# Probabilities times values of two attention heads by turns on the column halves of the TensorE array, 128 queries at a time

## The chip, the cores and the metric

The kernel runs on one core of one Trainium2 chip. The metric is the device time of one execution in microseconds (us). Less is better.

## The reference, cut to what matters

The program is two layers of a hybrid backbone over 256 latent tokens and 256 context tokens with 1024 features. Each layer feeds three token mixers from one projection: neighbourhood attention (8 heads of 64), a bidirectional recurrence, and windowed attention with a sink (8 query heads, 2 key heads). A mixture of 16 experts follows. The change touches the last two lines of the attentions, where probabilities meet values:

```python
p = jax.nn.softmax(jnp.concatenate([s_nb, s_ctx], axis=-1), axis=-1).astype(v.dtype)
o = (jnp.einsum('brjqam,brajmhd->brjqhd', p_nb, v_nb)      # neighbourhood keys
     + jnp.einsum('bhrjql,blhd->brjqhd', p[..., n_nb:], vc))  # context keys
...
o = (jnp.einsum('bnqkgd,bnmkd->bnqkgd', p[..., :nloc], vb)   # window, the same form
     + jnp.einsum('bkgnql,blkd->bnqkgd', p[..., nloc:nloc + L], vc))
```

In layer 0 the context tokens also attend among themselves; in layer 1 only the latents are needed.

## The kernel before, in words

Heads are taken in four pairs (`hp`) by `na_attend` (line 703) and `wa_attend` (line 772). For a pair, the queries and keys are transposed and split in two parts, and one PSUM bank `psd` (`po`, tag "d", one buffer) collects the pair's output: head 0 (`par` 0) on partitions 0 to 63, head 1 on 64 to 127. `attend` (line 627) does one head. For each of two tiles of 128 latent queries (`t`) it computes scores against 512 keys (line 625, in PSUM `psa`), the softmax on VectorE and ScalarE (`softmax_rows`, lines 586 to 592), four transposes of the probabilities `P` (line 639, in PSUM `pst`) and a ScalarE copy into half of `pT` (line 640). Then four products with the values follow (line 642): 64 columns of values are the stationary operand and 256 queries of `pT` move. In layer 0 the context queries come next, in two products of 256 queries (line 656). `split_out` reads the pair's bank. Both operands are plain float32, so a product is two matmul records in the profile, each with a weight load of its own.

```python
for c in range(4):
    PE.matmul(po[pp, 256:512], vfn(c), pT[:, c], start=c == 0, stop=c == 3, tile_position=(0, 64 * par))
```

`tile_position=(0, 64 * par)` puts the product on one half of the array's columns. The other half is unused meanwhile, since a head's products follow one another. Layer 1's experts use both halves by turns: at line 1459 the inner loop runs over the two halves `c`, with 64 stationary and 512 moving columns, and at line 356 the first modulation vectors use four quarters.

A scheduler orders each engine's instructions. It places parts of the big projections (lines 243 to 245, three passes for each product) between the steps of the attention, so that TensorE has work while a softmax is under way. TensorE takes its instructions in the written order. The neighbourhood bias of a pair is loaded by SP (line 721, eight transfers into four slices of `bm`) on the queue that also carries the weights (line 215), and GpSimd adds a mask (line 725).

Of the kernel before, what the change touches and what calls it, by code (L numbers as in the profile page):

```python
# [76 lines left out]
def kernel(es, tc, A, out, dbg=None):  # L77
# [19 lines left out]
    def banks(**n):  # L97
        """the eight banks of PSUM, shared out anew"""
        if "pool" in pb:
            pb["pool"].__exit__(None, None, None)  # L100
        pb["pool"] = tc.tile_pool(name="ps", bufs=1, space=PSUM)
        pb["tiles"] = pb["pool"].__enter__()
        pb["n"] = n
# [10 lines left out]
    def ps_a(shape=(128, 512)):  # L114
        return bank("a", shape)
# [16 lines left out]
    # products of zeros keep the tensor engine at its full clock where it has to wait  # L132
# [9 lines left out]
    # the table of exponentials, loaded while the transfers run  # L142
# [6 lines left out]
    # silu of the two conditioning vectors, padded to 32 columns  # L149
# [8 lines left out]
    # sums the four row groups of the first modulation vectors  # L158
# [3 lines left out]
    # lower bounds of the forget gates: columns (direction, depth, head)  # L162
# [22 lines left out]
    def slot_queue(*extra):  # L185
        """buffers for weights in the order of their use, the longest unused first"""
        wst.clear()
        wst.extend([(wp, "raw")] * RAW_BUFS + [(pool, tag) for pool, tag in extra for _ in range(nbuf[tag])])
# [10 lines left out]
    def later():  # L199
        """for transfers that shall not get ahead of the weights so far"""  # L200
        return tc.issue_after(loads[-1].ins)

    def spare(tag, shape, dt=F32):
        """a buffer for weights that holds something else from now on"""
# [47 lines left out]
    def ada_group(l, g):  # L252
        """2048 columns of both rows of silu(c) @ w_ada + b_ada, a step for each 128 rows of w_ada"""
# [39 lines left out]
    def rstd_of(dst, ssq, n):  # L293
        """dst = (ssq / n + eps) ** -0.5"""
# [5 lines left out]
    def norm_rows(pool, xt):  # L300
        """xt over its root mean square"""
# [8 lines left out]
    def start(hp, tp, consume):  # L310
        """the first layer's make_hT and its first product, one block of 128 features after the other, with the
        block's modulation"""
# [109 lines left out]
    def gemm_cols(l, hT, cols0, toks):  # L422
        """transposed outputs: one [128 columns, tokens] bank for each 128-column block"""
# [12 lines left out]
    # Blocks of h = 1, 2, 4, ... tokens are merged in pairs. K holds a key times the product of the forget  # L436
    # gates from the token to its block's edge, Q a query times the product from the block's other edge, so
    # that K . Q at level h is the decayed score across the pair's middle; no product ever exceeds one.
    def hgrn(l, hT, ybT, hg_, hg, vv, take_v):
        full = l == 0  # L440
        T0 = 0 if full else 256
        with hg_:
# [20 lines left out]
            # two heads by turns  # L463
# [5 lines left out]
    def hgrn_head(l, hT, ybT, hg, vv, gw, h, full, T0):  # L469
# [5 lines left out]
        # forward keys, then backward keys; backward queries, then forward ones; so that with two strides  # L475
        # left blocks' forward keys and right blocks' backward ones (and the opposite queries) are one operand
# [17 lines left out]
        # diagonal: q . (kf + kb)  # L494
# [7 lines left out]
        for lv in range(9):  # L502
# [27 lines left out]
            if True:  # L530
                n = 256 // hs
                m0 = T0 // (2 * hs)
                # left blocks take the factor of the right one and right blocks that of the left one
# [35 lines left out]
    def head_rstd(pool, src, nh, wide=True):  # L569
        """[128, nh] inverse root mean squares of the heads of one token tile"""  # L570
# [10 lines left out]
    def softmax_rows(s_in, bm, init, nsk, P):  # L581
        """P = exp(s + bm - max) / sum, rows on partitions; the sink's logit (nsk its negative) joins maximum and sum"""
        m = sm.tile([128, 4], F32, name="smx", bufs=6)
        flat = P if len(P.shape) == 2 else P.rearrange("p a k -> p (a k)")
        # P = -(s + bm), m[0] = -max
# [8 lines left out]
    # A head's 64 dimensions fill the 128 rows as high and low parts of the queries against the high (then the  # L594
    # low) parts of the keys twice: two float32r passes for all four products.
    def stack_q(pool, ps, T0):
        """ps [128, tokens] two heads' queries, transposed"""
# [9 lines left out]
    def stack_k(pool, k, c0):  # L607
        """two heads' keys from column c0 of k [128, token tile, columns]"""
# [18 lines left out]
    def attend(l, pool, qT, kT, par, bms, init, nsk, vfn, po):  # L627
        """one head; po [64, tokens] of the pair's bank"""
        full = l == 0
        pp = slice(64 * par, 64 * par + 64)  # L630
        pT = pool.tile([128, 4, 256], F32, name="pT", bufs=2)
        for t in range(2):
            ps = ps_a((128, 2, 256))
            score(ps.rearrange("p a k -> p (a k)"), qT, kT, 2 + t, 512)
            P = pool.tile([128, 2, 256], F32, name="P", bufs=3, tag="P")
            softmax_rows(ps, bms[t], init, nsk, P)
            pt = ps_t((128, 4, 128))
            for c in range(4):
                PE.transpose(pt[:, c], P[:, c // 2, 128 * (c % 2):128 * (c % 2) + 128], ident)
            S.copy(pT[:, :, 128 * t:128 * (t + 1)], pt)  # L640
        for c in range(4):
            PE.matmul(po[pp, 256:512], vfn(c), pT[:, c], start=c == 0, stop=c == 3, tile_position=(0, 64 * par))
        if full:
            ps = ps_a((128, 2, 256))
            P = pool.tile([128, 2, 256], F32, name="P", bufs=3, tag="P")
            for t in range(2):
                score(ps[:, t], qT, kT, t, 256)
                softmax_rows(ps[:, t], C[:, CZER:CZER + 256], init, nsk, P[:, t])
            pt = ps_t((128, 2, 2, 128))
            for c in range(2):  # L650
                for t in range(2):
                    PE.transpose(pt[:, c, t], P[:, t, 128 * c:128 * (c + 1)], ident)
            pT = pool.tile([128, 4, 256], F32, name="pT", bufs=2)
            S.copy(pT[:, 0:2], pt.rearrange("p c t q -> p c (t q)"))
            for c in range(2):
                PE.matmul(po[pp, 0:256], vfn(c), pT[:, c], start=c == 0, stop=c == 1, tile_position=(0, 64 * par))
# [37 lines left out]
    # 64 copies of a layer's bias table: a row of 3719 elements further on is one key column to the left  # L694
# [8 lines left out]
    def na_attend(l, pool, yT, q, k, v):  # L703
        full = l == 0
        T0 = 0 if full else 256
        bm = pool.tile([128, 5, 256], F32, name="bm")       # zeros for the context keys, then two heads' biases
        G.memset(bm[:, 0], 0.0)
        for hp in range(4):
# [6 lines left out]
            for par in range(2):  # L715
                h = 2 * hp + par
                b2 = []
                for t in range(2):
                    i = 1 + 2 * par + t
                    for r in range(2):  # L720
# [5 lines left out]
                    b2.append(mk(bm, 0, [[256 * i, 2], [1, 256]]))  # L726
                attend(l, pool, qT[par], kT[par], par, b2, 3e38, None,
                       lambda c, h=h: v[:, c, 64 * h:64 * h + 64], po)
            split_out(yT, hp, po[:, T0:])

    def wa_inputs(l, hT, pool):
# [25 lines left out]
        def take_q(t, ps):  # L757
            # heads h and h + 4, which read the two key heads, side by side
# [13 lines left out]
    def wa_attend(l, pool, yT, q, k, v):  # L772
# [7 lines left out]
        for hp in range(4):  # L780
# [5 lines left out]
            for par in range(2):  # L786
                h = hp + 4 * par
                attend(l, pool, qT[par], kT[par], par, bms, sk[:, h:h + 1], sk[:, h:h + 1],
# [906 lines left out]
```

## Time and profile before

| | us |
|---|---|
| median of three runs | 1803.81 (1800.16 to 1805.40) |
| profiled execution, span from the first to the last instruction | 1791.0 |
| median of the runs less that span (launch and end around it) | 12.8 |
| attention of layer 0 | 395 to 590 |
| attention of layer 1 | 1325 to 1475 |
| PE busy over the span | 1675.2 |
| DVE busy over the span | 1049.5 |

The profile gives no time of its own for what lies around the span of the profiled execution; the difference to the median of the runs stands for it. A busy row of PE counts a matmul until its last column has left the array, so neighbouring matmuls overlap in it. What a matmul holds up is read from the distance of starts.

### The profile page before, as it was taken

To read this page: it belongs to the slowest core of one execution; us is meant where nothing else is said; L and a number is where in the kernel's file an instruction comes from. 1 tells how busy PE (TensorE), PEld (TensorE's weight loads), DVE (VectorE), ACT (ScalarE), POOL (GpSimd) and SP (SyncE) were. 2 spreads that over 40 slices of the span, in tenths; PEclk is the share of its full clock that TensorE was granted. 3 is DMA by queue.
4 is the path that set the end of the run, shared out by engine and by line. 5 is a ranking of instruction groups with operands and counts; after the bars stand their busy time and mean duration, and the time that the engine had idled before them with its cause. 6 is when DMAs were issued, how large, how long until landed. Compare 5 with 4: busy or idle time off the path is not lost. (4 is left out here: it accounts for less than half of the span.)

```text
span 1791.0 us, 23658 instructions
## 1 busy us (share of the span) xinstructions
PE 1675.2 (94%) x8656; PEld 1218.1 (68%) x8657; DVE 1049.5 (59%) x1907; ACT 813.7 (45%) x1351; POOL 342.9 (19%) x343
## 2 busy tenths in 40 slices
PE   8999999999999999499999987999999999799997
PEld 4657677886676888477877765878877888433332
DVE  4328473447876345788888888588558766401101
ACT  3313332346676432377877874434456764201100
POOL 0003130322300134311321113133313202100000
PEclk8999999999999999699999997999999999899999
DMA  9795748432210455599999951432424348899996
GB/s 294 282 316 173 265 156 286 134 100 65 59 48 24 118 201 178 184 328 373 360 331 370 357 187 66 125 89 82 148 85 118 88 114 303 314 386 386 387 356 251
DMA packets 263549, 379.97 MB, mean 212 GB/s; under 512 B 33014, under 2 KB 129782, under 8 KB 257920
## 3 DMA queue, kind: packets, MB, share of 16 engines
q1 hardware_dynamic: 251920, 361.19, 59.7%
q10 hardware_dynamic: 7184, 9.42, 1.6%
q0 software_dynamic: 4320, 7.75, 1.3%
q8 instruction: 72, 1.18, 0.3%
q14 instruction: 53, 0.43, 0.1%
HBM read 370.48 MB, written 17.72 MB: 217 GB/s over the span
## 5 line engine op out<-in xcount | busy, mean ns | idle before, releaser
L232 DVE TENSOR_TENSOR wlo<-wraw,whi 128x1024 fp32r<-128x1024 f32 (+2 forms) x368 | 439.4, 1215 | 182.7 <-ACT whi L231 167.8
L231 ACT CAST whi<-wraw 128x1024 fp32r<-128x1024 f32 (+2 forms) x368 | 369.7, 1023 | 174.1 <-PE psg L245 74.2
L243 PE MATMUL psg<-hTh,whi 128*128 128x512 f32 (+1 forms) x576 | 205.9, 359 | 0.0
L244 PE MATMUL psg<-hTl,whi 128*128 128x512 f32 (+1 forms) x576 | 203.7, 354 | 0.0
L245 PE MATMUL psg<-hTh,wlo 128*128 128x512 f32 (+1 forms) x576 | 203.0, 354 | 0.0
L243 PE MATMUL psg<-whi,hTh 128*128 128x512 f32 (+1 forms) x392 | 148.3, 382 | 2.2 <-ACT hTh L373 2.1
L245 PE MATMUL psg<-whi,hTl 128*128 128x512 f32 (+1 forms) x392 | 148.1, 381 | 0.5 <-DVE hTl L404 0.5
L244 PE MATMUL psg<-wlo,hTh 128*128 128x512 f32 (+1 forms) x392 | 148.3, 379 | 0.0
L243 PEld LDWEIGHTS psg<-hTh,whi 128*128 128x128 f32 x576 | 108.5, 188 | 27.0 <-issue 9.5
L1459 PE MATMUL psg<-wraw,xT 128*64 128x512 f32 x512 | 120.5, 596 | 1.1 <-ACTq L1134 0.9
L245 PEld LDWEIGHTS psg<-hTh,wlo 128*128 128x128 f32 x576 | 108.3, 189 | 17.6 <-issue 5.0
L244 PEld LDWEIGHTS psg<-hTl,whi 128*128 128x128 f32 x576 | 108.6, 188 | 16.3 <-issue 4.1
L243 PE MATMUL psg<-whi,xh 128*128 128x512 f32 x256 | 102.0, 398 | 0.7 <-ACT xh L1384 0.7
L244 PE MATMUL psg<-wlo,xh 128*128 128x512 f32 x256 | 100.1, 391 | 0.0
L245 PE MATMUL psg<-whi,xl 128*128 128x512 f32 x256 | 99.7, 391 | 0.0
L243 PEld LDWEIGHTS psg<-whi,hTh 128*128 128x128 f32 x392 | 74.2, 189 | 19.4 <-ACT hTh L373 3.8
L1459 PEld LDWEIGHTS psg<-wraw,xT 128*64 128x64 f32 x512 | 37.3, 137 | 72.6 <-issue 68.7
L245 PEld LDWEIGHTS psg<-whi,hTl 128*128 128x128 f32 x392 | 74.1, 190 | 16.6 <-DVE hTl L404 1.7
L244 PEld LDWEIGHTS psg<-wlo,hTh 128*128 128x128 f32 x392 | 74.3, 190 | 12.5
L1463 ACT ACTIVATE act<-psg 128x256 f32<-128x256 f32 x16 | 6.1, 383 | 150.7 <-PE psg L1459 129.0
L831 POOL TENSOR_TENSOR mg<-mg,gates 128x512 f32<-128x512 f32 (+1 forms) x32 | 37.1, 1168 | 170.2 <-DVE gates L830 160.5
L587 ACT ACTIVATE P<-P,smx 128x512 f32<-128x512 f32 (+1 forms) x96 | 62.2, 649 | 12.1 <-DVE smx L586 11.3
(417 smaller groups left out, 3294.8 us busy)
## 6 DMA issues: line engine op xcount, KB each, us to landing
wraw<-in_w_down_dram SPq DMA_DIRECT2D x64, 1024.0 KB
wraw<-in_w_ada_dram SPq DMA_DIRECT2D x40, 1024.0 KB
wraw<-in_w_in_dram SPq DMA_DIRECT2D x144, 256.0 KB
wraw<-in_w_up_dram SPq DMA_DIRECT2D x32, 1024.0 KB
wraw<-in_w_gate_dram SPq DMA_DIRECT2D x32, 1024.0 KB
wraw<-in_w_gate_dram SPq DMA_DIRECT2D x64, 512.0 KB
wraw<-in_w_up_dram SPq DMA_DIRECT2D x64, 512.0 KB
wraw<-in_w_in_dram SPq DMA_DIRECT2D x24, 1024.0 KB
```

Of the source, the lines that this page charges most:

```text
L231: S.copy(hi[:, :, 0:n], r[:, 2 * j:2 * j + 2, 0:n])
L232: V.tensor_tensor(lo[:, :, 0:n], r[:, 2 * j:2 * j + 2, 0:n], hi.bitcast(F32)[:, :, 0:n], ALU.subtract)
L243: PE.matmul(ps, ah, bh, start=start, stop=False)
L244: PE.matmul(ps, ah, bl, start=False, stop=False)
L245: PE.matmul(ps, al, bh, start=False, stop=stop)
L587: S.activation(flat, flat, AF.Exp, scale=-1.0, bias=m[:, 0:1], accum_out=m[:, 2:3])
L831: G.tensor_tensor(dst, dst, sg[:, i], ALU.add)
L1459: PE.matmul(pgu[64 * c:64 * c + 64, :], xT[:, 2 * p + k, o:o + 64], r[:, :, k, 256 * c:256 * c + 256], start=p == 0 and k == 0, stop=p == ...
L1463: S.activation(a, pgu[:, 0:256], AF.Silu)
```

## The change

`attend` now does both heads of a pair. The loop over the query tile is outside and the loop over the heads inside; each head's tile has a `pT` of [128, 4, 128] (four buffers instead of two of twice the size). After both heads' copies, `values` issues the products chunk by chunk (`c`) with the two heads by turns, so that consecutive products stand on different column halves. A product now moves 128 queries instead of 256; the context products of layer 0 still move 256. The bias slices of a pair are all loaded ahead of `attend`. Scores, softmax, transposes and copies keep their number and shapes.

```diff
@@ -624,36 +624,43 @@
         for i in range(2):
             PE.matmul(ps, qT[:, 128 * t:128 * (t + 1)], kT[i][:, 0:n], start=i == 0, stop=i == 1)
 
-    def attend(l, pool, qT, kT, par, bms, init, nsk, vfn, po):
-        """one head; po [64, tokens] of the pair's bank"""
-        full = l == 0
-        pp = slice(64 * par, 64 * par + 64)
-        pT = pool.tile([128, 4, 256], F32, name="pT", bufs=2)
+    def attend(l, pool, qT, kT, bms, init, nsk, vfn, po):
+
+
+        def values(pTs, n, cols):
+            for c in range(n):
+                for par in range(2):
+                    PE.matmul(po[64 * par:64 * par + 64, cols], vfn(par, c), pTs[par][:, c], start=c == 0, stop=c == n - 1,
+                              tile_position=(0, 64 * par))
+
         for t in range(2):
-            ps = ps_a((128, 2, 256))
-            score(ps.rearrange("p a k -> p (a k)"), qT, kT, 2 + t, 512)
-            P = pool.tile([128, 2, 256], F32, name="P", bufs=3, tag="P")
-            softmax_rows(ps, bms[t], init, nsk, P)
-            pt = ps_t((128, 4, 128))
-            for c in range(4):
-                PE.transpose(pt[:, c], P[:, c // 2, 128 * (c % 2):128 * (c % 2) + 128], ident)
-            S.copy(pT[:, :, 128 * t:128 * (t + 1)], pt)
-        for c in range(4):
-            PE.matmul(po[pp, 256:512], vfn(c), pT[:, c], start=c == 0, stop=c == 3, tile_position=(0, 64 * par))
-        if full:
-            ps = ps_a((128, 2, 256))
-            P = pool.tile([128, 2, 256], F32, name="P", bufs=3, tag="P")
-            for t in range(2):
-                score(ps[:, t], qT, kT, t, 256)
-                softmax_rows(ps[:, t], C[:, CZER:CZER + 256], init, nsk, P[:, t])
-            pt = ps_t((128, 2, 2, 128))
-            for c in range(2):
+            pTs = []
+            for par in range(2):
+                ps = ps_a((128, 2, 256))
+                score(ps.rearrange("p a k -> p (a k)"), qT[par], kT[par], 2 + t, 512)
+                P = pool.tile([128, 2, 256], F32, name="P", bufs=3, tag="P")
+                softmax_rows(ps, bms(par, t), init(par), nsk(par), P)
+                pt = ps_t((128, 4, 128))
+                for c in range(4):
+                    PE.transpose(pt[:, c], P[:, c // 2, 128 * (c % 2):128 * (c % 2) + 128], ident)
+                pTs.append(pool.tile([128, 4, 128], F32, name="pT", bufs=4))
+                S.copy(pTs[par], pt)
+            values(pTs, 4, slice(256 + 128 * t, 384 + 128 * t))
+        if l == 0:
+            pTs = []
+            for par in range(2):
+                ps = ps_a((128, 2, 256))
+                P = pool.tile([128, 2, 256], F32, name="P", bufs=3, tag="P")
                 for t in range(2):
-                    PE.transpose(pt[:, c, t], P[:, t, 128 * c:128 * (c + 1)], ident)
-            pT = pool.tile([128, 4, 256], F32, name="pT", bufs=2)
-            S.copy(pT[:, 0:2], pt.rearrange("p c t q -> p c (t q)"))
-            for c in range(2):
-                PE.matmul(po[pp, 0:256], vfn(c), pT[:, c], start=c == 0, stop=c == 1, tile_position=(0, 64 * par))
+                    score(ps[:, t], qT[par], kT[par], t, 256)
+                    softmax_rows(ps[:, t], C[:, CZER:CZER + 256], init(par), nsk(par), P[:, t])
+                pt = ps_t((128, 2, 2, 128))
+                for c in range(2):
+                    for t in range(2):
+                        PE.transpose(pt[:, c, t], P[:, t, 128 * c:128 * (c + 1)], ident)
+                pTs.append(pool.tile([128, 2, 256], F32, name="pT", bufs=4))
+                S.copy(pTs[par], pt.rearrange("p c t q -> p c (t q)"))
+            values(pTs, 2, slice(0, 256))
...
@@ -714,7 +721,6 @@
             po = bank("d")
             for par in range(2):
                 h = 2 * hp + par
-                b2 = []
                 for t in range(2):
                     i = 1 + 2 * par + t
                     for r in range(2):
@@ -723,9 +729,9 @@
                                         [[3719, 64], [31, 4], [1, 64]]))
                     bl = bm[:, i].rearrange("p (r c) -> p r c", r=4)
                     G.tensor_tensor(bl, bl, mk(C, CNCM, [[0, 4], [1, 64]]), ALU.add)
-                    b2.append(mk(bm, 0, [[256 * i, 2], [1, 256]]))
-                attend(l, pool, qT[par], kT[par], par, b2, 3e38, None,
-                       lambda c, h=h: v[:, c, 64 * h:64 * h + 64], po)
+            attend(l, pool, qT, kT, lambda par, t: mk(bm, 0, [[256 * (1 + 2 * par + t), 2], [1, 256]]),
+                   lambda par: 3e38, lambda par: None,
+                   lambda par, c, hp=hp: v[:, c, 128 * hp + 64 * par:128 * hp + 64 * par + 64], po)
             split_out(yT, hp, po[:, T0:])
 
     def wa_inputs(l, hT, pool):
...
@@ -783,13 +789,12 @@
                 PE.transpose(pt[:, 128 * t:128 * (t + 1)], q[:, t - T0 // 128, 128 * hp:128 * (hp + 1)], ident)
             qT = stack_q(pool, pt, T0)
             po = bank("d")
-            for par in range(2):
-                h = hp + 4 * par
-                attend(l, pool, qT[par], kT[par], par, bms, sk[:, h:h + 1], sk[:, h:h + 1],
-                       lambda c, par=par: v[:, c, 64 * par:64 * par + 64], po)
+            sink = lambda par, hp=hp: sk[:, hp + 4 * par:hp + 4 * par + 1]
+            attend(l, pool, qT, (kT[0], kT[1]), lambda par, t: bms[t], sink, sink,
+                   lambda par, c: v[:, c, 64 * par:64 * par + 64], po)
             split_out(yT, hp, po[:, T0:])
 
```

Line 642 and 656 become line 633, the transposes of line 639 become line 645, those of line 652 line 660, and line 721 becomes 727.

How it moves the instructions on TensorE, layer 0, third head pair of the neighbourhood attention, from the first product with the values to the next head's or tile's. `psd` is the pair's output bank, `pT` the transposed probabilities, `nav` the values, `psg` a projection, `psa` scores, `pst` transposes. Before:

```order
L642 MATMUL psd_3112<-pT_3119,nav_2486 64x256 x4
L652 MATMUL pst_3170<-C_76,P_3155 128x128 x3
L639 MATMUL pst_3195<-C_76,P_3189 128x128 x4
L245 MATMUL psg_3753<-whi_3761,hTl_151 128x512
L656 MATMUL psd_3112<-pT_3175,nav_2486 64x256 x2
L639 MATMUL pst_3210<-C_76,P_3204 128x128 x4
L625 MATMUL psa_3220<-kTh_3106,qT_3092 128x256
L625 MATMUL psa_3220<-kTl_3107,qT_3092 128x256
L652 MATMUL pst_3236<-C_76,P_3221 128x128
L243 MATMUL psg_3753<-whi_3761,hTh_150 128x512
L244 MATMUL psg_3753<-wlo_3762,hTh_150 128x512
L642 MATMUL psd_3112<-pT_3185,nav_2486 64x256 x4
```

Now:

```order
L645 MATMUL pst_3160<-C_76,P_3154 128x128 x4
L645 MATMUL pst_3184<-C_76,P_3178 128x128 x4
L244 MATMUL psg_3791<-wlo_3856,hTh_150 128x512
L633 MATMUL psd_3122<-pT_3165,nav_2486 64x128
L633 MATMUL psd_3122<-pT_3149,nav_2486 64x128
L633 MATMUL psd_3122<-pT_3165,nav_2486 64x128
L633 MATMUL psd_3122<-pT_3149,nav_2486 64x128
L633 MATMUL psd_3122<-pT_3165,nav_2486 64x128
L633 MATMUL psd_3122<-pT_3149,nav_2486 64x128
L633 MATMUL psd_3122<-pT_3165,nav_2486 64x128
L645 MATMUL pst_3200<-C_76,P_3194 128x128 x4
L633 MATMUL psd_3122<-pT_3189,nav_2486 64x128
```

Before, one head's four products stand together, all on one half. Now the heads' `pT` alternate, but the first product of a tile has been issued alone earlier, as in the last row for the next tile; a tile's eight products are a lone one and a run of seven.

The same engine in layer 1, second pair, with the numbers left out. Before:

```order
L642 MATMUL psd<-pT,nav 64x256 x4
L639 MATMUL pst<-C,P 128x128 x8
L244 MATMUL psg<-wlo,hTh 128x512
L711 MATMUL pst<-C,naq 128x128 x2
L245 MATMUL psg<-whi,hTl 128x512
L642 MATMUL psd<-pT,nav 64x256 x4
L611 MATMUL pst<-C,nak 128x128 x4
```

Now:

```order
L633 MATMUL psd<-pT,nav 64x128 x7
L645 MATMUL pst<-C,P 128x128 x8
L245 MATMUL psg<-whi,hTl 128x512
L633 MATMUL psd<-pT,nav 64x128
L718 MATMUL pst<-C,naq 128x128 x2
L633 MATMUL psd<-pT,nav 64x128 x7
L611 MATMUL pst<-C,nak 128x128 x4
```

Two runs of four became, for each tile, one lone product and a run of seven. Over the program the products with the values stand in 47 unbroken runs before, and in 78 now: 46 in layer 0 and 32 in layer 1. For the latents there are 32 tiles of eight products: 30 of the form 1 + 7, and two in the first pair that stand as 1, 8, 7. The eight context groups of four products stand as 1 + 3 seven times and as 4 once. So 38 lone products stand apart.

On SP's queue, layer 1, the bias slices of the second pair and the weights beside them. Before:

```order
L721 DMA bm<-rp_dram_2466 64x4x64 x4
L215 DMA wraw<-in_w_in_dram 128x4x128
L721 DMA bm<-rp_dram_2466 64x4x64 x4
L215 DMA wraw<-in_w_in_dram 128x4x128 x3
L721 DMA bm<-rp_dram_2466 64x4x64 x4
L215 DMA wraw<-in_w_in_dram 128x4x128
```

Now:

```order
L727 DMA bm<-rp_dram_2466 64x4x64 x2
L215 DMA wraw<-in_w_in_dram 128x4x128
L727 DMA bm<-rp_dram_2466 64x4x64 x6
L215 DMA wraw<-in_w_in_dram 128x4x128 x6
L727 DMA bm<-rp_dram_2466 64x4x64 x2
L215 DMA wraw<-in_w_in_dram 128x4x128 x2
```

Transfers that came in fours, a head's at a time, now come as two and six, and the six stand ahead of the next weights.

## Rows read from the trace of the kernel before

**Rows 1.** The page, parts 1 and 2: busy us by engine, then 40 slices (tenths)

```profile
span 1791.0 us, 23658 instructions
...
PE 1675.2 (94%) x8656; PEld 1218.1 (68%) x8657; DVE 1049.5 (59%) x1907; ACT 813.7 (45%) x1351; POOL 342.9 (19%) x343
...
PE   8999999999999999499999987999999999799997
...
PEclk8999999999999999699999997999999999899999
```

**Rows 2.** Engine windows of both attention stretches: us, busy (instructions), granted clock, DMA share, GB/s

```profile
395.00:590.00 195.00, 191.31 (x971) 136.49 (x971) 143.86 (x397) 129.68 (x298) 30.73 (x28) 1.00 0.21 58
1325.00:1475.00 150.00, 144.14 (x923) 117.13 (x924) 111.16 (x255) 105.11 (x216) 31.30 (x30) 1.00 0.39 106
```

**Rows 3.** Waits of PE from 395 to 590: total us, times, longest us

```profile
PE pst L639 <- DVE P L592: 1.0, 2, 0.7
PE psd L656 <- ACT pT L654: 0.8, 2, 0.6
```

**Rows 4.** Waits of PE from 1325 to 1475

```profile
PE pst L639 <- DVE P L592: 3.3, 5, 1.9
```

**Rows 5.** Groups of PE matmuls by shape: records | busy us, mean ns | idle before

```profile
L1459 PE MATMUL psg<-wraw,xT 128*64 128x512 f32 x512 | 120.5, 596 | 1.1 <-ACTq L1134 0.9 <-ACT xT L1342 0.2
...
L639 PE MATMUL pst<-C,P 128*128 128x128 f32 x256 | 39.6, 281 | 5.3 <-DVE P L592 4.3 <-DVE smx L591 0.8
...
L642 PE MATMUL psd<-pT,wvv 128*64 128x256 f32 x128 | 31.1, 386 | 0.0
L642 PE MATMUL psd<-pT,nav 128*64 128x256 f32 x128 | 31.0, 386 | 0.1
...
L656 PE MATMUL psd<-pT,nav 128*64 128x256 f32 x32 | 8.6, 392 | 0.8 <-ACT pT L654 0.8
L656 PE MATMUL psd<-pT,wvv 128*64 128x256 f32 x32 | 8.6, 390 | 0.0
...
L356 PE MATMUL psa<-wraw,cT 128*32 128x256 f32 x64 | 5.3, 384 | 0.0
```

**Rows 6.** PE in order of time, layer 0: start us, busy us, instruction [idle before]

```profile
431.00 0.28 PE L625 MATMUL psa<-kTl,qT 128*128 128x256 f32 x1
431.22 1.94 PE L642 MATMUL psd<-pT,nav 128*64 128x256 f32 x8
433.09 0.55 PE L652 MATMUL pst<-C,P 128*128 128x128 f32 x3
433.48 0.60 PE L639 MATMUL pst<-C,P 128*128 128x128 f32 x4
...
434.91 1.08 PE L656 MATMUL psd<-pT,nav 128*64 128x256 f32 x4 [0.60 <-ACT pT L654]
435.92 0.66 PE L639 MATMUL pst<-C,P 128*128 128x128 f32 x4
```

**Rows 7.** PE in order of time, layer 1's experts

```profile
1620.08 0.28 PE L1337 MATMUL psg<-Mg,hh 128*128 128x256 f32 x1
1620.20 0.28 PE L1337 MATMUL psg<-Mg,hl 128*128 128x256 f32 x1
...
1622.21 4.08 PE L1459 MATMUL psg<-wraw,xT 128*64 128x512 f32 x18
```

**Rows 8.** The page, part 5: weight loads of the interleaved expert products

```profile
L1459 PEld LDWEIGHTS psg<-wraw,xT 128*64 128x64 f32 x512 | 37.3, 137 | 72.6 <-issue 68.7 <-ACTq L1134 1.8 <-ACT xT L1342 0.8
```

**Rows 9.** Engine windows, 1360 to 1380, in layer 1's neighbourhood attention

```profile
1360.00:1380.00 20.00, 17.10 (x96) 13.01 (x96) 17.25 (x35) 11.14 (x22) 7.70 (x7) 1.00 0.48 135
```

**Rows 10.** Waits of SP's queue, 1325 to 1475

```profile
SPq L721 <- DVE smx L586: 7.5, 10, 1.7
```

**Rows 11.** Groups by line: copies of the transposed probabilities

```profile
L640 ACT COPY pT<-pst 128x512 f32<-128x512 f32 x64 | 36.6, 586 | 28.9 <-PE pst L639 28.6
```

## The prediction

> **What bounds the kernel now.** I read the page first. TensorE is busy 94% of a span of 1791.0 us, and its slices from the 9th to the 14th and from the 30th to the 33rd, where the two attentions lie, stand at 9 at the full granted clock, 2.4 GHz [rows 1]. Then the engine windows of the two stretches: of 195 us in layer 0 PE is idle for 3.7, of 150 us in layer 1 for 5.9, while DVE is busy 74% of either and the DMA engines 21 and 39% [rows 2]. So the attention is paced by what TensorE is given to do, with projections filled in between the softmax steps. The waits agree: the largest named ones are 1.0 and 0.8 us in layer 0 and 3.3 us in layer 1 [rows 3, 4]. Microseconds taken off TensorE there should shorten the program, unless an instruction at its head has to wait instead.
>
> The products with the values are 128 + 128 + 32 + 32 = 320 records of 256 moving columns [rows 5]. Busy time overstates them, so I take distances of starts. A run of eight is busy for 1.94 us and a run of four for 1.08 [rows 6]: four more records cost 0.86, which is **0.215 us each**. Together 320 x 0.215 = 68.8 us.
>
> **Do two halves work at once?** The trace has this at other places. In layer 1's experts 18 records of 512 columns, by turns on two halves, are busy for 4.08 us [rows 7]. Less the last one's 0.60 [rows 5], eight steps of a pair take 3.48, or 0.435 each; one record of 512 columns alone would take 2 x 0.215 = 0.43. So the second half comes free. With four quarters, 64 records of 256 columns are busy for 5.3 us, 0.083 each [rows 5].
>
> **The change, part by part.**
>
> *Columns.* A latent product now has 128 columns. Four transposes, each a record of 128 columns, are busy for 0.60 us [rows 6] and one for 0.28 [rows 5]: a step is (0.60 - 0.28) / 3 = 0.107, and half of 0.215 is 0.108. I take 0.108. A product is two steps of its half. In a tile that stands as 1 + 7 the lone product takes two steps; the seven put four products on one half and three on the other, so eight steps: ten in all. Thirty such tiles make 300 steps, and the first pair (1, 8, 7) 2 + 8 + 8 = 18: 318 x 0.108 = 34.3 us. A context group as 1 + 3 takes 2 + 4 steps of 0.215, the one that stands as 4 takes four: 46 x 0.215 = 9.9. Sum 44.2 against 68.8: **24.6 us less**.
>
> *Entering and leaving a run.* From the score's start at 431.00 to the run of eight there are 0.22 us, where records of that shape follow each other in 0.12 [rows 6, 7]: 0.10 lost. From 431.22 to the next start at 433.09 there are 1.87, where eight records need 1.72: 0.15 lost, as with the run of four (434.91 to 435.92, 1.01 for 0.86). The three transposes behind it step by (0.55 - 0.28) / 2 = 0.135 instead of 0.107 [rows 5, 6]: 0.05 lost. That is 0.30 a run. There were 47 runs and there are 78, because each lone product is a run of its own: 31 x 0.30 = **9.3 us more**. Net 15.3 us less, 9.9 of it in layer 0 and 5.4 in layer 1 (columns 27.5 to 17.3, 16 runs more).
>
> *Weight loads.* There are 576 instead of 320, each with 64 columns as before. Two halves want 2 x 64 weight columns in a step of 0.108. The trace shows no interleaved records that short. The nearest row is a projection-like run that loads 128 weight columns for each matmul and steps by 0.12 [rows 7]. With 194 steps in which both halves run, that would cost 194 x 0.012 = 2.3 us; the other end is 0. I take **1.2**.
>
> *Where DVE paces.* From 1360 to 1380, within layer 1's neighbourhood attention, PE is idle 2.9 of 20 us and DVE busy 17.25 [rows 9]. Time taken off TensorE there turns into waiting. I give up half of layer 1's share: **2.7** (ends 0 and 5.4).
>
> *Added waits.* Each of the 31 new runs can wait for a copy of `pT`, 0.586 us on ACT [rows 11]. Spread over the 47 runs of before, the wait named at a product with the values, 0.8 us [rows 3], is 0.02 each; all idle time of PE in both stretches, 9.6 us [rows 2], would be 0.20. Projections still stand between copy and product, so I take the lower end, **0.6** (upper end 6.2).
>
> *The rest.* Scores, transposes, copies and softmax steps keep number and shape, so ACT and DVE get no work. SP's bias transfers wait 7.5 us for softmax steps in layer 1 [rows 10], and now six stand ahead of the next weights instead of four. I cost that at nothing, because PE's waits in these stretches end with DVE and ACT, none with a transfer [rows 3, 4]: projections already loaded cover it. Without that cover each late piece would cost PE up to the longest of SP's waits there, 1.7 us. The bank of a pair stays single, so the next pair still waits for `split_out`, as before.
>
> **Sum.** 24.6 - 9.3 - 1.2 - 2.7 - 0.6 = 10.8 us. The span should fall from 1791.0 to 1780.2. With the 12.8 us between the span and the median of the runs that is 1803.8 - 10.8 = **1793.0 us**. What follows the attentions starts that much earlier and should keep its length, since in layer 0 the DMA engines are nearly idle until then.
>
> **Rivals.**
>
> *The gain is spent on waits.* DVE paces all of layer 1 (its 5.4 us go), and layer 0 and 1 pay 0.20 for each of 31 runs: 15.3 - 5.4 - 6.2 = 3.7, so 1800.1 us. For it: DVE's 74% rises when PE gets shorter, and its chain has few gaps in layer 1. Against it: in layer 0, where two thirds of the gain lie, PE's waits were 2% of the time.
>
> *The second head comes late.* The run of seven needs the later head's `pT`, and TensorE takes nothing else meanwhile. At 38 places a lone product stands ahead of such a run. At the waits for DVE's probabilities in layer 1, 3.3 us in five [rows 4], a wait costs 0.66: 38 x 0.66 = 25.1 us, hence 1803.8 - 10.8 + 25.1 = 1818.1 us, slower than before. It decides from 10.8 / 38 = 0.28 us a place. For it: several of the runs stand only one projection pass behind the second head's transposes, and the copy takes 0.586. Against it: the same closeness before the change led to one wait of 0.6 at the group shown [rows 6] and 0.8 in all.
>
> *The halves don't overlap.* If short records by turns went one after the other, 512 x 0.108 + 64 x 0.215 = 69.1 us would stand against 68.8, and the runs would cost 9.3: 1813.4 us. Against it: the interleaved records of rows 5 and 7.
>
> *Weights are loaded only between matmuls.* A load of 64 columns lasts 0.137 us [rows 8]. If it could not run beside a matmul, steps would be 0.245 and 0.352: 318 x 0.245 + 46 x 0.352 + 9.3 - 68.8 = 34.6 us more, 1838 us. Against it: a pair's step of 0.435 has no room for 0.137 beyond its columns. The Trainium skill, page "TensorE: Matmul & The Clock Gate", section "Part 3: Packing small matmuls — row/col tiling", says that weight loads overlap running matmuls only when the row group differs, and two column halves share theirs. By that rule this rival would hold; the steps above disagree with it, though no run here shows it at 128 columns.
>
> **Chances.** The forecast 0.69; the gain spent on waits 0.14; the second head late 0.11; no overlap 0.03; weights between matmuls 0.03. A change within 0.3% (5.4 us) is about what a measurement cannot tell from none. So faster 0.69, same 0.14, slower 0.17. The range begins at 1783, about where runs cost half of their price and the other deductions vanish (24.6 - 4.7 = 19.9 us less), and ends at 1804, so as to hold the case of spent waits; it leaves out the slower ones.
>
> **What would show it.** Line 633: 576 records, the runs of seven busy for about 8 x 0.108 + 0.28 = 1.1 us, starts of two halves a few ns apart. The PE idle time in the attentions should stay below 14 us, and the first should be some 7 to 9 us shorter, the second 2 to 4. A wait of 0.3 us or more at most runs of seven would make me wrong; so would steps of 0.2 within a run, or an attention whose end has not moved.

## The result, and the profile after

The changed kernel takes 1782.55 us (median of four runs, 1782.28 to 1783.88) against 1801.99 (1799.27 to 1805.40) for the kernel before on the same chip: a ratio of 0.9894 [0.9879, 0.9909]. It is faster, by more than was forecast, and its time lies 0.45 us below the forecast's range of 1783 to 1804.

The page of the changed kernel, parts 1 and 2, for [rows 1]:

```profile
span 1780.5 us, 24184 instructions
...
PE 1663.4 (93%) x8912; PEld 1218.9 (68%) x8913; DVE 1047.0 (59%) x1907; ACT 816.7 (46%) x1353; POOL 345.9 (19%) x343
...
PE   8999999999999999599999987999999999799997
...
PEclk8999999999999999699999997999999999899999
```

The slices look nearly the same; PE has 256 records more and 11.8 us less busy time. Engine windows of the two stretches, for [rows 2]:

```profile
395.00:590.00 195.00, 189.98 (x1141) 140.96 (x1140) 144.86 (x401) 136.20 (x306) 31.84 (x28) 1.00 0.23 62
1325.00:1475.00 150.00, 144.38 (x1111) 125.03 (x1110) 115.70 (x256) 111.23 (x220) 34.42 (x37) 0.99 0.41 114
```

PE is idle for 5.0 and 5.6 us, where it was idle for 3.7 and 5.9: 1.0 us more waiting in the two together. The second stretch now has a granted clock of 0.99 instead of 1.00, which comes back below. Groups of PE matmuls by shape from 395 to 1475, for [rows 5]:

```profile
L633 PE MATMUL psd<-pT,wvv 128*64 128x128 f32 x256 | 24.3, 282 | 0.1
L633 PE MATMUL psd<-pT,nav 128*64 128x128 f32 x256 | 23.9, 282 | 0.0
...
L633 PE MATMUL psd<-pT,wvv 128*64 128x256 f32 x32 | 6.9, 398 | 0.1
L633 PE MATMUL psd<-pT,nav 128*64 128x256 f32 x32 | 6.5, 397 | 0.0
```

Those are 576 records, busy for 61.6 us against 79.3. PE in order of time, layer 0, for [rows 6]:

```profile
429.75 0.40 PE L243 MATMUL psg<-whi,hTh 128*128 128x512 f32 x1
430.07 0.43 PE L633 MATMUL psd<-pT,nav 128*64 128x128 f32 x2
...
434.27 1.09 PE L633 MATMUL psd<-pT,nav 128*64 128x128 f32 x14
435.29 0.66 PE L645 MATMUL pst<-C,P 128*128 128x128 f32 x4
435.87 0.43 PE L633 MATMUL psd<-pT,nav 128*64 128x128 f32 x2
436.23 0.39 PE L625 MATMUL psa<-kTh,qT 128*128 128x256 f32 x1
...
437.01 1.09 PE L633 MATMUL psd<-pT,nav 128*64 128x128 f32 x14
438.03 0.39 PE L625 MATMUL psa<-kTh,qT 128*128 128x256 f32 x1
```

A run of seven products (14 records) is busy for 1.09 us. Single records of the trace, which the view merges, show that within it the two halves start 6 to 7 ns apart; the first step takes 0.160 us, the others 0.109. A lone product is busy for 0.43 us and delays the score behind it to 0.36 us after its start.

Waits of PE (total us, times, longest us), from 395 to 590, for [rows 3], and from 1318 to 1470, for [rows 4]:

```profile
PE psa L625 <- ACT kTh L618: 1.5, 4, 0.6
PE psa L625 <- DVE kTl L619: 1.2, 1, 1.2
PE psa L625 <- DVE smx L586: 1.1, 1, 1.1
PE pst L645 <- DVE P L592: 0.5, 2, 0.3
...
PE psa L625 <- ACT kTh L618: 3.0, 3, 1.9
PE psa L625 <- DVE kTl L619: 1.6, 2, 1.1
```

No wait stands at a product with the values. The waits for probabilities are mostly gone; the late thing is now the split of a pair's queries and keys (`kTh`, `kTl`).

For the experiments I also read lengths from each trace. "Layer 0" and "layer 1" run from the first exponential of the layer's softmax (line 587) to the first ScalarE cast for the output projection behind its mixers, and hold its attention; the other two columns are what lies between and behind. "Half-clock time" is the time at a granted clock of 0.5 (1.2 GHz; at all other times it is 1.0, 2.4 GHz). For an execution without a trace it is 2 x (1 - mean clock) x span.

| trace | layer 0 | between | layer 1 | to the end | span | half-clock time, us |
|---|---|---|---|---|---|---|
| before, first trace | 230.5 | 698.5 | 155.1 | 307.8 | 1791.0 | 86.8 |
| `before_again` | 231.1 | 698.4 | 156.0 | 310.0 | 1792.8 | 88.5 |
| `look1` | 231.1 | 702.6 | 156.2 | 311.9 | 1802.3 | 96.6 |
| `look2` | 231.0 | 698.0 | 154.0 | 310.3 | 1792.8 | 87.0 |
| `look3` | 231.1 | 704.1 | 154.5 | 308.8 | 1798.9 | 99.6 |
| `look4` | 230.8 | 696.8 | 154.4 | 308.8 | 1793.4 | 82.2 |
| after | 222.6 | 698.1 | 149.0 | 309.8 | 1780.5 | 91.7 |
| `after_again` | 223.0 | 702.5 | 149.7 | 310.6 | 1784.7 | 91.8 |

### The profile page after: what moved, and what is told of

It is laid out like the page before. It is cut to its first block, busy times and chain, and to the rows that moved or that the text cites. A ratio compares the mean times of both kernels' runs of the same rounds, so it can differ in the third digit from the quotient of the medians.

```text
span 1780.5 us, 24184 instructions
## 1 busy us (share of the span) xinstructions
PE 1663.4 (93%) x8912; PEld 1218.9 (68%) x8913; DVE 1047.0 (59%) x1907; ACT 816.7 (46%) x1353; POOL 345.9 (19%) x343
## 5 line engine op out<-in xcount | busy, mean ns | idle before, releaser
L245 PE MATMUL psg<-whi,xl 128*128 128x512 f32 x256 | 99.6, 390 | 0.0
```

Of the source, the lines that this page charges most:

```text
L245: PE.matmul(ps, al, bh, start=False, stop=stop)
```

## The experiments

The first theory: the costs and gains on TensorE were sized rightly, and the forecast began from a wrong base, since the 12.8 us "around the span" belong to no place around it. Its rivals lie in the terms: the halves, the layers, the 128 queries.

### The kernel before again, five executions with a trace

No edit. The first was run twelve times, the others once each.

> The kernel of before, unchanged. Theory 1 (the prediction started from the wrong base): its executions differ in length inside the span, and what lies around a span is about 2 us, as in the changed kernel (1782.55 for a span of 1780.5); so the times of 1799 to 1805 have spans of 1797 to 1803, and an execution with a span of 1791.0 takes 1793. Theory 2: 9 to 13 us lie around each span of this kernel, and its spans stand near 1791 whatever the time.

> The kernel before, unchanged, one execution with its trace. Theory: executions differ by spells in which the granted clock is 0.5, so a longer span than the 1791.0 us of the first trace goes with spells that the first trace has not, each of at least 3.4 us, about 0.4 us of span per us of them; layer 1's attention takes 155 us without a spell in it and 1.5 to 2 us more with one. Rival: the same spells as in the first trace, and the time is lost in waits for transfers.

> The kernel before, unchanged, a second execution with its trace. Theory: the same 155 us in layer 1's attention if no spell at clock 0.5 lies in it, 156.5 to 157 with one; the span 1791 to 1808 us, in the order of the time spent at 0.5. Rival: spans differ by more than 5 us between traces with the same spells.

> The kernel before, unchanged, a third execution with its trace. Theory: as in the second, the span follows the time spent at clock 0.5, and layer 0's attention, in which no trace so far has a spell, stays at 230.5 to 231.1 us. Rival: layer 0's attention varies too, by more than 1 us.

> The kernel before, unchanged, a fourth execution with its trace. Theory: the span follows the time spent at clock 0.5, the time of the run is the span and 2 to 3 us. Rival: the time of the run stands more than 5 us above the span of the same execution.

Measured: `before_again` 1800.78 us (1794.90 to 1804.33), ratio 0.9997 [0.9978, 1.0016]; the looks 1804.72, 1794.89, 1801.04 and 1795.29. In all 61 executions of this kernel beside the experiments the time is the span and 1.9 to 3.1 us. So the 12.8 us were not there. The first trace's own time is not on record; with a span of 1791.0 it ran, by this, in 1792.9 to 1794.1, at the low end of the 61 (1793.52 to 1807.98, median 1801.04). One of them has a shorter span, 1790.4.

What makes executions differ is in part the clock. In a line through the 61 the span grows by 0.39 us for each us of half-clock time (correlation 0.77). The looks show a place. The engine window 915 to 935, in layer 0's experts, of `look1`:

```profile
915.00:935.00 20.00, 18.37 (x81) 15.18 (x80) 12.12 (x13) 12.32 (x17) 3.28 (x5) 0.83 0.77 274
```

and of `look2`:

```profile
915.00:935.00 20.00, 18.18 (x92) 14.62 (x91) 14.71 (x16) 14.70 (x19) 6.16 (x6) 1.00 0.86 292
```

TensorE's work there in order of time, in `look1`:

```profile
922.22 0.33 PE L1435 MATMUL pst<-C,M 128*128 128x128 f32 x1 [1.34 <-POOL M L1433]
...
926.89 0.63 PE L244 MATMUL psg<-wlo,ah 128*128 128x512 f32 x1
927.32 0.63 PE L243 MATMUL psg<-whi,ah 128*128 128x512 f32 x1
...
930.26 0.39 PE L244 MATMUL psg<-wlo,ah 128*128 128x512 f32 x1
930.49 0.39 PE L245 MATMUL psg<-whi,al 128*128 128x512 f32 x1
```

and in `look2`:

```profile
919.06 0.33 PE L1435 MATMUL pst<-C,M 128*128 128x128 f32 x1 [1.34 <-POOL M L1433]
...
923.02 0.40 PE L243 MATMUL psg<-whi,ah 128*128 128x512 f32 x1
923.25 0.40 PE L244 MATMUL psg<-wlo,ah 128*128 128x512 f32 x1
...
924.87 0.39 PE L245 MATMUL psg<-whi,al 128*128 128x512 f32 x1
```

The same instructions after the same wait of 1.34 us: in one execution 6.8 us at 0.5 follow, in which a pass of 512 columns takes 0.43 us from start to start instead of 0.23, in the other none. From one side of it (922.22 against 919.06) to the other (930.49 against 924.87) `look1` falls 2.5 us further behind `look2`. Set side by side instruction by instruction, the two traces part at three more such places, where `look1` has a spell that `look2` lacks or has shorter: 1.6 us near 698, 1.6 near 1384 and 2.3 near 1722, the last with 0.6 us of longer waits in it. The four make 7.9 of the 9.5 us between the two spans. Not every step is the clock alone: at 108 us `look3` has a spell and falls 2.6 us behind `look2`, but TensorE waits 2.09 us for weights from DRAM just before it, where it waits 0.93 in `look2`.

The theory held in its main part: layer 0's attention stays within 0.6 us, and layer 1's takes 154.0 to 155.1 us without a spell and 156.0 to 156.2 with one. In its strict form it failed: the span does not follow the half-clock time in order (`look3` has 3.0 us more of it than `look1` and is 3.4 us shorter). The clock is a part of the scatter, in `look1` against `look2` most of it; transfers have a part too, by the wait at 108 us. How much of the scatter over all 61 is theirs stays open: no run tried them by themselves.

### The change again

> The changed kernel, unchanged. Both theories: 1782 to 1784, and 2 us around the span. Theory 1 also expects that its spans differ by less than those of the kernel before.

Measured: 1785.51 us (1782.52 to 1789.86, six runs), ratio 0.9906 [0.9880, 0.9932]. The gain repeats; the median lies 1.5 us above what was expected, so the four runs of the result stood at the low end here too. All ten runs of the change have a median of 1783.86, against 1801.04 for the 61 before: 17.2 us. With every span set to 90 us of half-clock time by the slope above (**"at equal clock"** from here on), the means are 1798.2 and 1783.8: 14.4 us. I use that measure to compare terms of a few us, not less: the mean of 6 to 12 executions is uncertain by 0.3 to 1.0 us (its standard error), and the kernel before stands at 1798.0 on the chip of this section, `heads_apart` and `whole`, and at 1798.7 on that of the other edits. Against the kernel before on the same chip the change gains 13.4 here. The measure also takes out what a kernel's own order does to the clock, if it does anything.

### The heads one after the other

```diff
-            for c in range(n):
-                for par in range(2):
+            for par in range(2):
+                for c in range(n):
```

> The changed kernel with a head's products together: all chunks of head 0, then of head 1, also 128 queries at a time. If the halves' overlap is the gain, a tile takes 16 steps of 0.108 instead of 10, a context group 8 steps of 0.215 instead of 6: 31 x 0.65 + 7 x 0.43 = 23 us more than the changed kernel, 1806. If the new order of the softmax steps was the gain, 1782 to 1785.

Measured: 1805.16 us (1801.70 to 1810.50, twelve runs), ratio 1.0022 [1.0005, 1.0038]; at equal clock 21.0 us above the change and 6.6 above the kernel before. PE in order of time:

```profile
432.92 1.09 PE L633 MATMUL psd<-pT,nav 128*64 128x128 f32 x8
433.94 0.51 PE L625 MATMUL psa<-kTl,qT 128*128 128x256 f32 x2
```

Four products of one head take the 1.09 us in which the change does seven of two heads. The overlap of the halves carries the whole gain, and the change without it costs time, as the third rival said.

### One layer alone

For `layer0_alone` layer 1 goes through the code of before (`attend_one`, the former `attend`); for `layer1_alone` layer 0 does, with `if not l:`.

```diff
     def attend(l, pool, qT, kT, bms, init, nsk, vfn, po):
+        if l:
+            for par in range(2):
+                attend_one(l, pool, qT[par], kT[par], par, [bms(par, t) for t in range(2)], init(par), nsk(par),
+                           lambda c, par=par: vfn(par, c), po)
+            return
...
```

> The changed attention in layer 0 alone; layer 1 is as before. By the count of steps and runs layer 0 holds 9.9 of 15.3 us, and in the traces its part from the first softmax to the merged branches went from 230.5 to 222.6, 7.9 less: 1792 to 1794 against 1801 of the kernel before. If the gain came from a spot in layer 1, 1801.

> The changed attention in layer 1 alone. The count gives 5.4 us, the traces 155.1 to 149.0, 6.1 less: 1795 to 1796. The prediction's deduction (half of it lost where DVE paces) gives 1798. The two single layers should add up to the whole change.

Measured: layer 0 alone 1791.90 us (1788.67 to 1795.09, eight runs), ratio 0.9954 [0.9936, 0.9971], at the lower end of what was expected. Layer 1 alone 1792.04 (1786.26 to 1798.66, twelve runs), ratio 0.9948 [0.9932, 0.9964], a larger gain than any expectation. At equal clock they are 7.8 and 7.0 us below the kernel before, together 14.8 for the change's 14.4: within the uncertainty the layers add, and layer 1 gives about as much as layer 0. The two traces allow a closer look at layer 1's attention, for each has 6.8 us at half clock in it: it takes 152.8 us in `layer1_alone` and 158.6 in `layer0_alone`, 5.8 less.

### 256 queries by turns

```diff
+        pTs = [pool.tile([128, 4, 256], F32, name="pT", bufs=2) for par in range(2)]
         for t in range(2):
-            pTs = []
...
-                pTs.append(pool.tile([128, 4, 128], F32, name="pT", bufs=4))
-                S.copy(pTs[par], pt)
-            values(pTs, 4, slice(256 + 128 * t, 384 + 128 * t))
+                S.copy(pTs[par][:, :, 128 * t:128 * (t + 1)], pt)
+        values(pTs, 4, slice(256, 512))
...
-                pTs.append(pool.tile([128, 2, 256], F32, name="pT", bufs=4))
+                pTs.append(pool.tile([128, 4, 256], F32, name="pT", bufs=2)[:, 0:2])
```

> The heads by turns, but 256 latent queries at a time as before: the products wait for both query tiles of both heads. 44 runs instead of 78, and about as many column steps (154 x 0.215 = 33.1 us for 34.3): by count 34 x 0.30 + 1.2 = 11.4 us less than the changed kernel, 1772 to 1774. Rival: the products come late and in one block, with less to fill the waits, and pT's two buffers hold up the next copies: 1785 or more.

Measured: 1789.34 us (1786.31 to 1795.87, eight runs), ratio 0.9942 [0.9923, 0.9961]. It has 44 runs of products instead of 78, and the 11.4 us that the count gave are not there; the rival's 1785 or more came true. At equal clock it is 1.8 us above the change, which is not clear of the noise; a further 3.7 us go with its half-clock time, 96.6 us against 87.0. Counting runs alone misleads: with the products of a pair in one lump layer 0's attention is shorter in the trace (219.4 us for 222.8), but layer 1's is longer (154.8 for 149.4), and PE is idle for 11.1 us from 1325 to 1475 instead of 5.6. Its waits there:

```profile
PE psa L625 <- ACT kTh L618: 4.4, 3, 2.0
PE pst L645 <- DVE smx L591: 1.4, 1, 1.4
PE psa L625 <- DVE smx L586: 1.3, 2, 1.1
```

### A tile's products in one run

The scheduler had issued the first head's first product alone. Here the later head goes first and the others follow it: 40 runs. `whole_wide` does this with 256 queries: 24 runs.

```diff
+            first = None
             for c in range(n):
-                for par in range(2):
-                    PE.matmul(po[64 * par:64 * par + 64, cols], vfn(par, c), pTs[par][:, c], start=c == 0, stop=c == n - 1,
-                              tile_position=(0, 64 * par))
+                for par in (1, 0):
+                    with tc.issue_after(first.ins) if first else nullcontext():
+                        r = PE.matmul(po[64 * par:64 * par + 64, cols], vfn(par, c), pTs[par][:, c], start=c == 0, stop=c == n - 1,
+                                      tile_position=(0, 64 * par))
+                    first = first or r
```

> Each tile's products stand in one run, the later head first, so that no lone product stands apart: 40 runs in place of 78. If runs and steps cost what the prediction counted, 38 x 0.30 = 11.4 us go, and the lone steps with them, 31 x 0.216 + 7 x 0.43 = 9.7: 21 us less than the changed kernel, 1761, or 1766 if a quarter is lost to the softmax's pace. Rival: the lone products only fill time in which TensorE would wait for the second head, and 1780 to 1784 stays.

> Both edits: 256 queries at a time and no lone product, 24 runs. By count 54 x 0.30 = 16.2 us and lone steps of 13 x 0.43 + 7 x 0.43 = 8.6 less than the changed kernel, 1761; if waits take what the runs give, as they took 13 of 21 us where runs were kept whole, about 1775.

Measured: `whole` **1778.19 us** (1775.27 to 1784.82, six runs), ratio 0.9872 [0.9845, 0.9898]. It beats both kernels, but misses the 1761 and 1766 that were expected; at equal clock it is 7.9 us below the change. `whole_wide` 1788.28 (1783.72 to 1790.34, six runs), ratio 0.9928 [0.9907, 0.9950]: a miss by 13 us of the nearer expectation, with 105.4 us of half-clock time. In its trace 13.6 us of that lie in layer 1's attention, which takes 157.6 us, longer than before the change. At equal clock it would stand between the change and `whole`, but its own six runs follow a flatter line (0.21 us for each us), so that figure is loose.

Why `whole` gives less than half of what the count said: a full run costs what the run of seven did, PE in order of time,

```profile
433.15 1.09 PE L635 MATMUL psd<-pT,nav 128*64 128x128 f32 x16
434.18 0.66 PE L648 MATMUL pst<-C,P 128*128 128x128 f32 x4
```

so the lone product and its run are saved, but PE waits more: it is idle for 9.3 and 12.3 us in the two stretches, 11.0 more than in the change, about the missing half of the 21. From 395 to 590 and from 1325 to 1475:

```profile
PE psa L625 <- ACT kTh L618: 2.3, 4, 1.1
PE pst L663 <- DVE P L592: 1.8, 3, 0.8
...
PE psa L625 <- ACT kTh L618: 5.6, 4, 2.6
PE pst L648 <- DVE P L592: 2.7, 4, 1.5
PE psg L244 <- DVE wlo L232: 2.4, 1, 2.4
```

In layer 0 the stretch shrinks from 222.8 to 215.4 us, in layer 1 from 149.4 to 146.5 only, and this trace has no spell at half clock there, where both traces of the change have one: there the waits for ACT and DVE, which the prediction looked for in the change, begin with this version.

## Why the prediction was wrong, point by point

**Two steps failed: the base, and the deduction where DVE paces** (below). The base: "With the 12.8 us between the span and the median of the runs that is 1803.8 - 10.8". The 12.8 us were taken for launch and end, a constant. About 2.1 us are; the rest was the distance between one execution at the low end and the middle of a scatter of 14 us. So 1803.8, the median of three, was no firm start, and the range hung on it too: its low end is 1803.8 - 19.9 = 1783.9, stated as 1783; from the 1801.0 of all 61 the same sum gives 1781.1, and the measured time lies inside. The table ahead of the prediction had already put the 12.8 us down to launch and end. The forecast of the span, 1780.2, met the trace's 1780.5 by luck: both are executions at the low end of their scatter, and the terms between them were off by some us. The 10.45 us between 1793.0 and 1782.55 divide so: 2.8 because three runs before had a median of 1803.8 and 61 have 1801.0; 3.6 because the gain at equal clock is 14.4 and not 10.8; 2.8 more in the medians of all runs (17.2 against 14.4), of which the smaller half-clock time of the change, 87.0 against 91.0 us on average, makes 1.5; 1.3 because the four runs of the result lie below the median of ten. The range let only the terms vary. It left no room for what executions do to two medians.

**Columns, 24.6 us less: held.** Steps of 0.109 us were forecast as 0.108, the run of seven as 1.1 us and measured as 1.09, and the heads one after the other cost 21.0 us. What [rows 7] showed at 512 columns holds at 128.

**Entering and leaving, 0.30 a run: held.** A run starts 0.32 to 0.33 us after a projection record of 512 columns (429.75 to 430.07 above), where those follow one another in 0.23: 0.10. Its first step takes 0.05 us more than the others. The transposes behind it start 0.204 us after its last record instead of 0.109, and the second of them 0.165 after the first: 0.10 and 0.05. The net of 15.3 stands against 14.4 at equal clock.

**Weight loads, 1.2: not there.** PE's weight loads of line 633 by shape:

```profile
L633 PEld LDWEIGHTS psd<-pT,nav x288: 132/137/137, 404.6 to 1398.3; 128*64 128x64 f32 x144
```

Two loads of 0.137 us go with each step of 0.109, and the step is that of one half alone (0.109 in `heads_apart`). The lower end, 0, was the right one. The rule of the Trainium skill, page "TensorE: Matmul & The Clock Gate", section "Part 3: Packing small matmuls — row/col tiling", that a weight load overlaps a running matmul only when the row group differs, does not agree with this: the halves share their rows, and loads longer than a step cost nothing.

**Where DVE paces, 2.7: wrong.** PE's idle time from 1325 to 1475 is 4.9 to 5.9 us in the six traces before and 5.6 and 6.3 in the two of the change, so little of what was taken off TensorE turned into waiting. Layer 1's part shrank by 5.2 us between executions without and with a spell there, by 6.7 between those with one; alone it gave 7.0 at equal clock and 5.8 in the stretch. That is about the whole of its net 5.4 or more; why it can be more stays open. The window of 20 us [rows 9] was read as a bound: PE was idle in it mostly in one wait of 1.9 us for the probabilities [rows 4], and in the new order that wait is gone and one of 1.9 us for `kTh` stands elsewhere, 38 us behind the first exponential where the old one stood 49 behind it, so the sum of idle time nearly stayed. The second attention was to be 2 to 4 us shorter, and is 5 to 7. Layer 0, forecast at 7 to 9, gave 8.1 us in its stretch and 7.8 alone, less than its net 9.9.

**Added waits, 0.6: too low, within their upper end of 6.2.** PE's idle time in both stretches rose from 9.6 to 10.6 us between the first traces, and from 9.3 to 11.1 in the means of all, 1.8 more; it stays below the 14 that were set as a bound, and no named wait stands at line 633. In layer 0 before, the largest named wait was not the 1.0 us that the prediction names but one of 1.1 in all at the context transposes (line 652). The second rival, the late second head, is not seen: the scheduler left a projection pass or transposes between copy and product.

**The clock** was not in the prediction. Both traces of the change have 3.4 us at 0.5 in layer 1's attention; two of the six traces before have. PE in order of time in the changed kernel:

```profile
1359.41 0.50 PE L625 MATMUL psa<-kTh,qT 128*128 128x512 f32 x1 [1.89 <-ACT kTh L618]
...
1360.40 0.41 PE L245 MATMUL psg<-hTh,wlo 128*128 128x256 f32 x1
1360.62 0.41 PE L243 MATMUL psg<-hTh,whi 128*128 128x256 f32 x1
...
1363.75 0.28 PE L245 MATMUL psg<-hTh,wlo 128*128 128x256 f32 x1
1363.86 0.28 PE L243 MATMUL psg<-hTh,whi 128*128 128x256 f32 x1
```

Behind a wait of 1.89 us a pass of 256 columns takes 0.21 us instead of 0.11 to 0.12. In the traces before, such a spell is worth some 1.6 us in layer 1. The wait alone does not bring it about: before the change a wait of 1.9 us stands in layer 1's attention in executions with and without a spell, and `whole` waits 2.6 us there and has none. What does was not tried.

## What to carry to other kernels

Matmuls with 64 stationary columns leave half of the array free, and another head's products by turns on the other half came at no cost in columns here; keep each group in one unbroken run, as `whole` does, but do not gather more for it: two tiles in one run made longer waits. Sum a forecast against several executions, not one: compare the profiled execution with the lowest run, and leave room in the range for the scatter of both medians. Where executions differ, compare the granted clock first, and set small effects at equal clock.

## What was not expected of the hardware

- On one core too, executions of one kernel spread over 14 us (1793.5 to 1808.0), in part in steps where a spell at 1.2 GHz appears or not behind the same instructions and the same wait: 2.5 us in `look1` near 923 us, 1.2 in `look3` near 927.
- Records on two column halves start 6 to 7 ns apart with 128 columns each, and 0.137-us weight loads for both are hidden in steps of 0.109 us.
- A run of seven interleaved products and one of eight are both busy for 1.09 us: the longer half, with eight records, sets it.
